# Two pages of values requested together and multiplied back to back in a paged decode

## The chip, the cores and the metric

The kernel runs on one core of a Trainium2 chip. A core has five engines with queues of their own: TensorE (PE, matmuls), VectorE (DVE), ScalarE (ACT), GpSimd (POOL) and SyncE (SP). Each engine takes its instructions in the order of its queue and waits at semaphores for the others. GpSimd and SyncE also issue DMAs here; 16 DMA engines move the data. The metric is the device time of one execution in microseconds.

## The reference

One inference step of a hybrid decoder layer (depth 1, float32), for a prompt of 1024 rows and for 8 samples with one new row each, which share the weights (model width 1024):

```python
q, k, v, logf, u, z = mixer_inputs(rmsnorm(x, g_mix), w_in, b_f, g_sgu_v)
x = x + merge_heads(attention(q, k, v, logf), sgu(u, z, w_s, b_s), g_att_out, g_sgu_out, w_o)
x = x + cross_attend(rmsnorm(x, g_cross), mem_k, mem_v, w_cq, w_co)      # 4 heads, 256 memory rows
x = x + conv_ffn(rmsnorm(x, g_ffn), prev, w_up, conv_w, conv_b, w_down)  # width 2816, gated
y = rmsnorm(x, g_final)
```

The part that matters is the attention of the samples. Each sample has a past of 8192 rows in a paged cache: 64 pages of 128 rows, 8 heads of 64, for keys and for values, 268 MB in all for 8 samples. With the cumulated forget gates as a bias, it is

```python
k_all = concat([k_pool[page_table].reshape(B, past, H, hd), k], axis=1)
v_all = concat([v_pool[page_table].reshape(B, past, H, hd), v], axis=1)
p = softmax(einsum('bqhd,bkhd->bhqk', q, k_all) * hd ** -0.5 + c_q - c_k)
out = einsum('bhqk,bkhd->bqhd', p, v_all)
```

## The kernel before

The prompt's work is the main line. It goes through its stages one after the other (projections, attention, merge and cross-attention "mid", gated MLP "ffn"; the later ones in two halves of 512 rows). Its matmuls are float32 products made from three products of a split (lines 271 to 273), 128 x 512 each.

The samples' work is a second line, `sample()`: first `decode()`, the paged attention, then `sample_rest()`, the samples' own merge, cross-attention and MLP. Both lines are Python generators. The main loop at the end of `build` takes a step of the prompt, adds its weight to a count, and hands out a step of the samples for each `PACE` of that count (`PACE` depends on the stage: 20.0 in the first half's attention, 8.5 in its MLP, 2.5 in the second MLP). So the program order mixes the two. A planner then orders every engine's queue by a simulated time line, with all waits and buffers. `behind(ENG.PE)` adds the edge that the instructions inside may not come ahead of the newest TensorE instruction of the prompt's steps so far (`last`); `tc.issue_after(ins)` is the same for an instruction that is named, and `newest(ENG.PE)` is the TensorE instruction that was written last.

In `decode()` the loop over `g` has 148 steps. A "page" is here one load of 128 partitions x 2048 floats, 1 MB, a sixteenth of a sample's keys or values (4 rows of 512 in each partition). In step `g`, `b, ch = divmod(g, 16)`:

- `kstep(b, ch, ...)` (lines 1338 to 1358): GpSimd requests a page of keys (line 1341, an indirect DMA into a tile of the pool `kv`), VectorE multiplies it by the query (line 1347) and sums within heads into the scores `s` (line 1351).
- At the sample's end come the softmax pieces (`soft_max`, `soft_all`, `soft_exp`, `soft_sum`), spread over the first steps of the next sample.
- `vstep(b, ch, ...)` (lines 1397 to 1415), 18 steps behind the keys (16 and `VLAG` = 2): GpSimd requests a page of values (line 1400, into the same pool `kv`), and a closure `mm` is returned. `mm` multiplies the page (line 1406): four matmuls, one for each of the four rows `j` of a partition, with 32 columns of weights (4 x 8 scores), each in its own group of 32 columns of the array (`tile_position`) and its own 32 partitions of the PSUM tile `dv`, 512 wide. All 16 pages of a sample accumulate into `dv`.
- `vmask` and `vend` take the sum out of `dv`.

The pool `kv` has `NKV` = 4 buffers for keys and values together; whoever asks next gets the buffer that comes free. `dv` has one buffer. The closures wait in the list `pend`. When it holds `VB` = 2, both are called in the step after, the earlier page first, each behind the newest instruction of the prompt; nothing ties the second to the first. In each step one page of values is requested, after the closures that were called in it. So GpSimd's queue alternates: a page of keys, a page of values, a page of keys.

The weights of the prompt come over SyncE's queue into four buffers `wr`; after the decode the samples' weights come over GpSimd's queue into `kv`.

Of the kernel before, what the change touches and what calls it, by code (L numbers as in the profile page):

```python
# [15 lines left out]
ENG = mybir.EngineType  # L16
# [33 lines left out]

NKV = 4
VLAG = 2
VB = 2
MIXR = 1.0
G0R = 0.0
WH = 5
# [23 lines left out]
def build(nc, tc, ctx, a, phases=None):  # L80
# [43 lines left out]
    def KV():  # L124
        return dpool.tile([P, 2048], F32, tag="kv", bufs=NKV, name=nm("kv"))
# [33 lines left out]
    def D2(n=512, dt=F32):  # L159
        return dpool.tile([P, 512], dt, tag="d2", bufs=5, name=nm("d2"))[:, :n]  # L160
# [168 lines left out]
    def newest(e):  # L329

        return next(i for i in reversed(nc.cur_bb.bb.instructions) if i.engine == e)
# [952 lines left out]
    def behind(e):  # L1284

        return tc.issue_after(last[e]) if e in last else nullcontext()


    def decode():
# [77 lines left out]
        def soft_all(b, pm):  # L1367
            ps = MS()
            with behind(ENG.PE):
                nc.tensor.transpose(ps[:8, :P], pm, ident)  # L1370
            with tc.high_priority():
                m1 = sm([8, 1], "m1", 2)
                nc.vector.tensor_reduce(m1, ps[:8, :P], axis=AX.X, op=ALU.max)
                nc.vector.tensor_tensor(mT[:, b : b + 1], m1, snT[:, b : b + 1], op=ALU.max)
                dg = sm([8, 8], "dg", 2)
                nc.vector.tensor_scalar(dg, ident[:8, :8], mT[:, b : b + 1], None, op0=ALU.mult)
            return dg
# [13 lines left out]
        def soft_sum(b, lp):  # L1391
            ps = MS()
            with behind(ENG.PE):
                mmul(ps[:8, :1], lp, ones[:, 0:1], start=True, stop=True)
            nc.vector.tensor_copy(lT[:, b : b + 1], ps[:8, :1])

        def vstep(b, ch, st, dv):
            s = st[1]
            kv = KV()
            nc.gpsimd.indirect_dma_start(kv, None, a["cache_v"], off(kidx[:, b, ch : ch + 1]))  # L1400
            kvv = kv.rearrange("p (k c) -> p k c", c=512)

            def mm():
                with behind(ENG.PE):
                    for j in range(4):
                        mmul(  # L1406
                            dv[32 * j : 32 * j + 32, :],
                            s[:, ch * 4 : ch * 4 + 4, :].rearrange("p k h -> p (k h)"),
                            kvv[:, j, :],
                            start=(ch == 0),  # L1410
                            stop=(ch == 15),
                            tile_position=(0, 32 * j),
                        )

            return mm

        def vmask(b, dv):
            vm = D2()
            with tc.high_priority():
                nc.vector.tensor_tensor(  # L1420
                    vm.rearrange("p (h d) -> p h d", d=64),
                    dv.rearrange("p (h d) -> p h d", d=64),
                    dm8.unsqueeze(2).broadcast_to((P, 8, 64)),
                    op=ALU.mult,
                )
            return vm

        def vend(b, vm):
            ps = MS()
            with behind(ENG.PE):  # L1430
                mmul(ps[:1, :], ones[:, 0:1], vm, start=True, stop=True)
            row = D2()[:1]
            nc.vector.tensor_copy(row, ps[:1, :])
            nc.sync.dma_start(att_d[b : b + 1, :], row)
# [3 lines left out]
        st, A, dt_, pm, dg, lp, dv, vm = ([None] * 8 for _ in range(8))  # L1438
        pend = []
        st[0] = prep(0)  # L1440
        for g in range(8 * 16 + 16 + VLAG + 2):
            b, ch = divmod(g, 16)
            if ch == VLAG + 1 and 2 <= b < 10:
                vend(b - 2, vm[b - 2])
            if ch == 0 and 1 <= b < 9:
                dg[b - 1] = soft_all(b - 1, pm[b - 1])
            if ch == 1 and 1 <= b < 9:
                lp[b - 1] = soft_exp(b - 1, st[b - 1], dg[b - 1])
            if ch == 2 and 1 <= b < 9:
                soft_sum(b - 1, lp[b - 1])  # L1450
            if b < 8:
                kstep(b, ch, st[b])
                if ch == 11:
                    A[b] = gates_scan(b)
                if ch == 13:
                    dt_[b] = gates(b, A[b])
                if ch == 14 and b < 7:
                    st[b + 1] = prep(b + 1)
                if ch == 15:
                    pm[b] = soft_max(b, st[b], dt_[b])  # L1460
            if len(pend) == VB:

                for vb_, vch_, f in pend:
                    f()
                pend.clear()
                if vch_ == 15:
                    vm[vb_] = vmask(vb_, dv[vb_])
            vb, vch = divmod(g - 16 - VLAG, 16)
            if 0 <= vb < 8:
                if vch == 0:  # L1470
                    dv[vb] = DV()
                pend.append((vb, vch, vstep(vb, vch, st[vb], dv[vb])))
            yield 1


# [446 lines left out]
```

## Time and profile before

| | |
|---|---|
| Median of 3 runs | 1874.07 us (1871.21 to 1876.5) |
| The profiled execution | 1881.57 us |
| Its span, first to last instruction | 1879.7 us |
| TensorE busy | 1802.3 us, 96% |
| VectorE, ScalarE, GpSimd busy | 74%, 40%, 26% |
| Granted TensorE clock, mean | 0.982 |
| HBM traffic | 276 GB/s over the span |
| Pages of values multiplied | from 195.8 to 1469.0 us of the span |

How to read the rows: a row of the time line has the start and the length in us, the engine, the line, the operation, the tiles (out<-in), the shapes and the count (neighbours of one kind are merged); in brackets is how long the engine was idle before it and what released it. A row of a stage has its ends, its length, the busy time of each engine (with the count of instructions), the granted clock, the share of time the DMA engines were busy, and GB/s. Groups have, behind the bar, busy time, mean ns of one, and idle time before. A matmul of float32 operands (line 1406) takes two passes and leaves two records. PE is a matmul, PEld the load of its weights, POOLq a queue's own waits.

### The profile page before, as it was taken

What the parts mean: (1) busy time and instruction counts of PE and PEld (TensorE: products, weight loads), DVE (VectorE), ACT (ScalarE), POOL (GpSimd) and SP (SyncE); (2) the same over time, 40 slices, a digit from 0 to 9 for tenths busy, and PEclk for the clock granted to TensorE, in tenths of its full rate; (3) what the DMA queues carried; (4) which work ended last, traced back from release to release, by engine and by line L of the source; (5) the groups of instructions that cost most, each with busy time, mean ns of one, the idle gap of its engine ahead of it and who ended that gap; (6) DMA issues with size and microseconds to landing.
All of it is one profiled execution on the core that took longest, in us unless ns stands there. A gap on an engine that the chain in (4) does not pass through costs nothing.

```text
span 1879.7 us, 24248 instructions
## 1 busy us (share of the span) xinstructions
PE 1802.3 (96%) x9239; PEld 1291.7 (69%) x9239; DVE 1394.2 (74%) x1664; ACT 750.9 (40%) x1363; POOL 480.0 (26%) x437
## 2 busy tenths in 40 slices
PE   8999989878998999999999999999999999999998
PEld 5987666556676667776777776765675668667765
DVE  4788668776687787989989998897965549654344
ACT  6332356565633435333324234235353334232232
POOL 1232333331122332313422323334322111101110
PEclk9999999889998999999999999999999999999999
DMA  8877888784496876759877888889859577667971
GB/s 320 286 261 271 324 324 297 243 263 167 169 376 216 329 268 249 298 197 363 314 274 301 302 316 324 347 325 340 325 220 359 193 282 263 253 219 276 331 246 59
DMA packets 157012, 521.27 MB, mean 277 GB/s; under 512 B 20808, under 2 KB 40520, under 8 KB 124128
## 3 DMA queue, kind: packets, MB, share of 16 engines
q0 software_dynamic: 57168, 341.14, 49.1%
q1 hardware_dynamic: 92816, 165.99, 25.7%
q10 hardware_dynamic: 6912, 12.59, 1.8%
q8 instruction: 73, 1.20, 0.2%
q14 instruction: 43, 0.35, 0.1%
HBM read 495.73 MB, written 23.93 MB: 276 GB/s over the span
## 4 chain that ended last, share of the span: by engine, by line
PE 83%; DVE 5%; DMA 4%; ACT 3%; issue 3%; POOL 1%; SPq 0%; DVEq 0%; POOLq 0%; ACTq 0%
PE ba L271 13%; PE ba L272 12%; PE ba L273 12%; PE bb L271 7%; PE bb L272 7%; PE bb L273 7%; PE dv L1406 6%; DVE kv L1347 1%; PE dv L1656 1%; PE ba L1002 1%; PE ba L1004 1%; DMA kv<-cache_k,kidx 1%; PE bb L788 1%; DVE s L1351 1%; PE ba L1003 1%
## 5 line engine op out<-in xcount | busy, mean ns | idle before, releaser
L234 ACT ACTIVATE wh<-wr 128x1024 fp32r<-128x1024 f32 (+2 forms) x220 | 228.7, 1044 | 518.2 <-PE ba L272 168.5
L235 DVE TENSOR_TENSOR wl<-wr,wh 128x1024 fp32r<-128x1024 f32 (+2 forms) x220 | 262.8, 1200 | 134.0 <-PE ba L273 55.4
L1347 DVE TENSOR_TENSOR kv<-kv,d 128x1024 f32<-128x1024 f32 (+1 forms) x184 | 295.8, 1633 | 24.3 <-DMA kv<-cache_k,kidx 23.6
L1341 POOL DMA_INDIRECT kv<-cache_k,kidx x128 | 177.0, 1383 | 535.0 <-DVE s L1351 262.2
L1351 DVE TENSOR_REDUCE s<-kv 128x16 f32<-128x1024 f32 (+1 forms) x184 | 296.3, 1624 | 0.2
L1400 POOL DMA_INDIRECT kv<-cache_v,kidx x128 | 173.3, 1354 | 404.7 <-DVE s L1351 180.0
L271 PE MATMUL ba<-wh,u 128*128 128x512 f32 (+1 forms) x601 | 229.6, 383 | 4.3 <-DVE u L961 2.5
L272 PE MATMUL ba<-wl,u 128*128 128x512 f32 (+1 forms) x601 | 227.5, 379 | 0.0
L273 PE MATMUL ba<-wh,u 128*128 128x512 f32 (+1 forms) x601 | 224.9, 379 | 0.0
L272 PE MATMUL ba<-u,wh 128*128 128x512 f32 (+2 forms) x520 | 203.1, 391 | 0.0
L271 PE MATMUL ba<-u,wh 128*128 128x512 f32 (+2 forms) x520 | 202.7, 391 | 0.2 <-DVE u L238 0.2
L273 PE MATMUL ba<-u,wl 128*128 128x512 f32 (+2 forms) x520 | 202.1, 389 | 0.0
L271 PE MATMUL bb<-u,wh 128*128 128x512 f32 (+2 forms) x344 | 138.9, 404 | 1.1 <-DVE u L238 1.1
L271 PEld LDWEIGHTS ba<-wh,u 128*128 128x128 f32 x601 | 113.3, 189 | 38.2 <-issue 9.6
L272 PE MATMUL bb<-u,wh 128*128 128x512 f32 (+2 forms) x344 | 137.5, 401 | 1.6 <-DVE u L238 1.6
L1406 PE MATMUL dv<-kv,s 128*32 128x512 f32 x1024 | 135.2, 614 | 3.0 <-DMA kv<-cache_v,kidx 3.0
L273 PE MATMUL bb<-u,wl 128*128 128x512 f32 (+2 forms) x344 | 136.9, 398 | 0.0
L273 PEld LDWEIGHTS ba<-wh,u 128*128 128x128 f32 x601 | 113.0, 188 | 26.7 <-issue 5.0
L272 PEld LDWEIGHTS ba<-wl,u 128*128 128x128 f32 x601 | 113.3, 189 | 22.4 <-issue 1.7
L272 PEld LDWEIGHTS ba<-u,wh 128*128 128x128 f32 x520 | 98.5, 189 | 32.3 <-issue 12.2
L271 PEld LDWEIGHTS ba<-u,wh 128*128 128x128 f32 x520 | 98.3, 190 | 31.5 <-issue 8.4
L273 PEld LDWEIGHTS ba<-u,wl 128*128 128x128 f32 x520 | 98.2, 189 | 27.7 <-issue 8.1
(426 smaller groups left out, 3048.8 us busy)
## 6 DMA issues: line engine op xcount, KB each, us to landing
wr<-w_up SPq DMA_DIRECT2D x88, 512.0 KB
kv<-w_up POOLq DMA_DIRECT2D x22, 1024.0 KB
wr<-w_down SPq DMA_DIRECT2D x40, 512.0 KB
kv<-w_down POOLq DMA_DIRECT2D x11, 1024.0 KB
wr<-w_in SPq DMA_DIRECT2D x16, 512.0 KB
wr<-w_o SPq DMA_DIRECT2D x16, 512.0 KB
wr<-w_cq SPq DMA_DIRECT2D x16, 512.0 KB
wr<-w_co SPq DMA_DIRECT2D x16, 512.0 KB
```

What stands on the lines that cost most here:

```text
L234: nc.scalar.activation(h, src, AF.Copy)
L235: nc.vector.tensor_tensor(l, src, h.bitcast(F32), op=ALU.subtract)
L271: mmul(out, sh, mh, start=(i == 0), stop=False)
L272: mmul(out, sh, ml, start=False, stop=False)
L273: mmul(out, sl, mh, start=False, stop=(i == n - 1))
L788: nc.tensor.transpose(tr[:, c * P : (c + 1) * P], p_[:, kt * P : (kt + 1) * P], ident)
L1002: mmul(pss[i], mh[k][:, tb], wh, start=(k == korder[0]), stop=False)
L1341: nc.gpsimd.indirect_dma_start(kv, None, a["cache_k"], off(kidx[:, b, ch : ch + 1]))
L1347: nc.vector.tensor_tensor(kvv[:, i : i + m, :], kvv[:, i : i + m, :], qb.unsqueeze(1).broadcast_to((P, m, 512)), op=ALU.mult)
L1351: nc.vector.tensor_reduce(s[:, ch * 4 + i : ch * 4 + i + m, :].rearrange("p k h -> p (k h)"), kvv[:, i : i + m, :].rearrange("p k (h d) -> ...
L1400: nc.gpsimd.indirect_dma_start(kv, None, a["cache_v"], off(kidx[:, b, ch : ch + 1]))
L1406: mmul(dv[32 * j : 32 * j + 32, :], s[:, ch * 4 : ch * 4 + 4, :].rearrange("p k h -> p (k h)"), kvv[:, j, :], start=(ch == 0), stop=(ch == ...
```

## The change

`VB` goes. A page pair is now requested in one step: in every second step (`vch` odd) `vstep` is called for pages `vch - 1` and `vch`, one after the other, behind the step's page of keys. In the next step the list is emptied from its end: the later page is multiplied first, behind the newest instruction of the prompt as before, and the earlier page then with an edge to the TensorE instruction just written, the last matmul of the later page. The accumulation in `dv` therefore begins with page 1 and ends with page 14. `dv` is taken in the step in which pages 0 and 1 are requested, and the mask follows pages 15 and 14. The step in which a pair is multiplied is the same as before; page `vch - 1` is requested one step later than before.

```diff
-VB = 2
...
-            def mm():
-                with behind(ENG.PE):
+            def mm(after=None):
+                with tc.issue_after(after) if after else behind(ENG.PE):
                     for j in range(4):
                         mmul(
                             dv[32 * j : 32 * j + 32, :],
                             s[:, ch * 4 : ch * 4 + 4, :].rearrange("p k h -> p (k h)"),
                             kvv[:, j, :],
-                            start=(ch == 0),
-                            stop=(ch == 15),
+                            start=(ch == 1),
+                            stop=(ch == 14),
                             tile_position=(0, 32 * j),
                         )
...
-            if len(pend) == VB:
-
-                for vb_, vch_, f in pend:
-                    f()
-                pend.clear()
-                if vch_ == 15:
-                    vm[vb_] = vmask(vb_, dv[vb_])
+            if pend:
+
+                pend.pop()()
+                pend.pop()(newest(ENG.PE))
+                if vch == 15:
+                    vm[vb] = vmask(vb, dv[vb])
             vb, vch = divmod(g - 16 - VLAG, 16)
-            if 0 <= vb < 8:
-                if vch == 0:
+            if 0 <= vb < 8 and vch % 2:
+                if vch == 1:
                     dv[vb] = DV()
-                pend.append((vb, vch, vstep(vb, vch, st[vb], dv[vb])))
+                pend += [vstep(vb, c, st[vb], dv[vb]) for c in (vch - 1, vch)]
             yield 1
```

## The prediction

> **What bounds the kernel now.** I read the page first (busy time, the chain that ended last, the costliest groups), then busy time by stage, then TensorE's own instructions in order of time around the multiplication of a page of values (line 1406), then GpSimd's requests.
>
> ```profile
> PE 1802.3 (96%) x9239; PEld 1291.7 (69%) x9239; DVE 1394.2 (74%) x1664; ACT 750.9 (40%) x1363; POOL 480.0 (26%) x437
> PE 83%; DVE 5%; DMA 4%; ACT 3%; issue 3%; POOL 1%; SPq 0%; DVEq 0%; POOLq 0%; ACTq 0%
> L1406 PE MATMUL dv<-kv,s 128*32 128x512 f32 x1024 | 135.2, 614 | 3.0 <-DMA kv<-cache_v,kidx 3.0
> ...
> 840.00:960.00 120.00, 120.00 (x550) 85.95 (x550) 108.91 (x97) 37.12 (x56) 40.64 (x27) 1.00 0.85 319
> 960.00:1060.00 100.00, 100.00 (x471) 71.65 (x468) 92.19 (x84) 33.60 (x50) 28.32 (x22) 1.00 0.80 298
> 1160.00:1300.00 140.00, 134.57 (x676) 95.59 (x675) 124.11 (x149) 53.85 (x101) 51.48 (x36) 1.00 0.88 330
> 1380.00:1470.00 90.00, 89.20 (x476) 56.94 (x475) 47.02 (x75) 39.55 (x68) 19.75 (x23) 1.00 0.81 300
> ```
>
> TensorE is busy in 96% of the span and holds 83% of the last chain. In the stage rows the columns after the length are busy PE, PEld, DVE, ACT, POOL, then granted clock, DMA share, GB/s. PE is full from 840 to 1060, nearly full from 1380 to 1470, and lacks 5.4 us from 1160 to 1300. So in most of the time of the decode what TensorE saves comes off the end. The 1024 records of line 1406 are 128 pages of 8 records (four column groups, two passes each), and only 3.0 us of PE idle time stand before them: pages of values practically always arrive in time.
>
> **What the change does on TensorE.** The old code also multiplies two pages in one step, but it does not tie them together. A page that is multiplied alone, and two that stand together:
>
> ```profile
> 847.46 0.40 PE L272 MATMUL ba<-wl,u 128*128 128x512 f32 x1
> 847.78 1.07 PE L1406 MATMUL dv<-kv,s 128*32 128x512 f32 x8
> 848.78 0.50 PE L273 MATMUL ba<-wh,u 128*128 128x512 f32 x1
> 849.12 0.39 PE L271 MATMUL ba<-wh,u 128*128 128x512 f32 x1
> 849.35 0.40 PE L272 MATMUL ba<-wl,u 128*128 128x512 f32 x1
> ...
> 1010.98 0.39 PE L273 MATMUL ba<-u,wl 128*128 128x512 f32 x1
> 1011.30 1.92 PE L1406 MATMUL dv<-kv,s 128*32 128x512 f32 x16
> 1013.15 0.51 PE L271 MATMUL bb<-u,wh 128*128 128x512 f32 x1
> 1013.49 0.40 PE L272 MATMUL bb<-u,wh 128*128 128x512 f32 x1
> ```
>
> Full-array matmuls start 0.23 us apart (849.12 to 849.35). From 847.46 to 849.12 are 1.66 us with one of them and one page between; two ordinary steps would be 0.46, so a page alone costs 1.20. From 1010.98 to 1013.49 are 2.51, so two together cost 2.05. Two alone cost 2.40: each joining saves 0.35 us, the entry into the narrow shape and the way out of it that are gone.
>
> How many pages stand alone shows in the busy time of this line by stage (PE, then PEld):
>
> ```profile
> 1160.00:1300.00 140.00, 17.05 (x128) 2.52 (x128) 1.00 0.88 330
> 1300.00:1400.00 100.00, 11.46 (x80) 1.57 (x80) 0.98 0.82 309
> 1400.00:1470.00 70.00, 18.80 (x144) 3.05 (x144) 1.00 0.84 311
> ...
> 202.52 1.06 PE L1406 MATMUL dv<-kv,s 128*32 128x512 f32 x8
> 1468.52 1.07 PE L1406 MATMUL dv<-kv,s 128*32 128x512 f32 x8
> ```
>
> From 1160 to 1300, 17.05 us for 16 pages is 1.066 each: all alone. From 1400 to 1470, 14 pages alone (14.9 us) and two pairs (3.9 us) make the 18.80. Over all stages the order of time has 73 groups of one page (the first and last are quoted), 24 of two, one of three, and two pairs that a small matmul cuts: 102 groups. After the change the two pages of a step are tied, which leaves 64. So 38 joinings by 0.35 us are **13.3 us of TensorE time**. Of the 73 single groups 35 lie between 760 and 1160 and after 1400, where PE is full or nearly so: 17 joinings, 6 us, that must show. The other 38 lie where PE lacks some per cent (3.9% from 1160 to 1300), and beside small matmuls the switch is a little cheaper. Since even there PE is busy nearly all the time I take **12 us** and keep 6 and 13.3 as bounds.
>
> **The order of the multiplications.** The later page first: PE waits once, for the page that lands last, and the other is there. The flags that open and close the accumulation move with it (pages 1 and 14). No instruction is added or removed, so 0. The masking after page 15 stays behind the same step: 0.
>
> **The requests.** These stand in GpSimd's queue. Now they alternate, keys, values, keys, values; afterwards keys, keys, values, values. 128 requests of each stay, so the issue costs nothing new. What moves is when each is made:
>
> ```profile
> 849.15 0.95 POOL L1400 DMA_INDIRECT kv<-cache_v,kidx  x1 [5.17 <-PE dv L1406]
> 855.21 1.09 POOL L1400 DMA_INDIRECT kv<-cache_v,kidx  x1 [1.93 <-PE dv L1406]
> 863.84 3.12 POOL L1400 DMA_INDIRECT kv<-cache_v,kidx  x1 [0.82 <-PE dv L1406]
> ...
> 871.10 0.94 POOL L1400 DMA_INDIRECT kv<-cache_v,kidx  x1 [0.89 <-PE dv L1406]
> ...
> 1012.66 0.94 POOL L1400 DMA_INDIRECT kv<-cache_v,kidx  x1 [7.63 <-PE dv L1406]
> 1013.91 0.94 POOL L1341 DMA_INDIRECT kv<-cache_k,kidx  x1 [0.30 <-issue]
> 1015.15 0.94 POOL L1400 DMA_INDIRECT kv<-cache_v,kidx  x1 [0.30 <-DVE s L1351]
> 1031.35 0.94 POOL L1400 DMA_INDIRECT kv<-cache_v,kidx  x1 [5.96 <-PE dv L1406]
> ```
>
> A request of values waits for the multiplication that frees a buffer. Where pages are multiplied alone, two requests take 14.7 us (849.15 to 863.84) or 15.9 (855.21 to 871.10); where they already go in pairs, 18.7 us (1012.66 to 1031.35), with the two requests 2.5 us apart. So the old kernel already runs stretches in nearly the new pattern, and PE is as full there. The first page of a pair loses its head start; the price on PE is nothing as long as the planner puts the pair where the later page has landed.
>
> The request of keys that stood behind the first page of values no longer waits for it. All waits of VectorE for keys are 23.6 us; two that stood on the chain that ended last are shown below the total:
>
> ```profile
> L1347 DVE TENSOR_TENSOR kv<-kv,d 128x1024 f32<-128x1024 f32 (+1 forms) x184 | 295.8, 1633 | 24.3 <-DMA kv<-cache_k,kidx 23.6
> ...
> 605.82 2.36 DVE L1347 TENSOR_TENSOR kv<-kv,d 128x1024 f32<-128x1024 f32 x2 [4.00 <-DMA kv<-cache_k,kidx]
> 623.67 1.22 DVE L1347 TENSOR_TENSOR kv<-kv,d 128x1024 f32<-128x1024 f32 x1 [4.33 <-DMA kv<-cache_k,kidx]
> ```
>
> I bound the effect on keys by these two waits, 8.3 us, to either side (they come earlier in GpSimd's queue, but the next two stand behind a pair of values that waits for PE). I take 0, because nothing says which side it falls to. SP's queue (the weights) is not touched; two pages of values in a row, 2 MB, can hold a load of weights back for a moment, which the four raw buffers cover.
>
> **Sum.** The profiled execution took 1881.57 us (span 1879.7), 0.4% above the median of 1874.07. 1881.57 - 12 = 1869.6, a ratio of 0.9936, and by the median 1862 us.
>
> **Rivals.** *Decode falls behind (slower).* With both pages requested together, the loop of a pair is the 13.3 us from request to multiplication (849.15 to its page at 862.47), plus the spacing of requests 1.25 (1012.66 to 1013.91), plus 1.9 for the pair and 1.4 to the next request: 17.8 us, and up to 3.3 more for the second page's transfer (1.05 MB at the 319 GB/s of that stage).
>
> ```profile
> 862.47 1.07 PE L1406 MATMUL dv<-kv,s 128*32 128x512 f32 x8
> ...
> 1848.10 1.02 PE L1709 MATMUL ms<-d,cp 128*8 128x512 f32 x2
> ...
> 1871.66 0.40 PE L273 MATMUL ba<-wh,u 128*128 128x512 f32 x1
> ```
>
> Against 15.9 now, some 30 of the 36 pairs that now run singly lose 2 us or more each, 60 us of delay for the samples. Their last multiplication is at 1848.10 and the prompt's at 1871.66, so 23.6 us are covered; with the 12 gained it decides at 36 us of delay, 1.2 us per pair. If the rest of the samples' path makes up 20 of the 60, then 60 - 20 - 23.6 - 12 is about +4, and if it makes up nothing, +24: I price it at +14, **1888**. For it: the arithmetic above. Against it: the samples' steps are handed out by the prompt's progress, so the loop of 18.7 us from 1012 to 1031 is already fast enough; and from 1470 on the DMA engines have room.
>
> ```profile
> 1470.00:1600.00 130.00, 130.00 (x591) 96.20 (x590) 92.02 (x124) 46.35 (x75) 20.75 (x33) 1.00 0.69 241
> ```
>
> The Trainium skill (Trainium Kernel Development and Optimization, Best Practices) asks for double buffers so that transfers run beside the computing; by it, a pair that holds two of the four buffers until both are multiplied loses that overlap and this rival would come true. The trace does not agree where pairs run now: between 1012.66 and 1031.35 keys are fetched beside the pair. For the second page's transfer the skill (DMA: Bandwidth & Descriptors, Anatomy of one DMA) gives 2.0 us + bytes/436e3, so 2.4 us by that page for one more, which would put the loop at 20.2 us instead of 21.1; no row here times a page's transfer alone.
>
> *TensorE waits for the later page (slower).* TensorE runs in order, so a page that lands after its place in the order stops the prompt's work too.
>
> ```profile
> 1311.44 1.87 PE L1406 MATMUL dv<-kv,s 128*32 128x512 f32 x8 [3.05 <-DMA kv<-cache_v,kidx]
> ```
>
> This is the only such wait now. At 3.05 us each it decides from 4 pairs of 64; with 8 it would be 24 - 12 = +12, **1886**. Against it: one in 128 pages now.
>
> *The gain is covered (same).* Only the joinings in full stages count, 6 us, and a little is lost in other places: -3, **1871**.
>
> **Chances.** The forecast 0.56 (its own range 1855 to 1868, from 6 us to 12 us and half of the 8.3 us on keys more or less); decode behind 0.20; waits of TensorE 0.11; covered 0.13. A measurement of this kernel can tell about 0.3%, 5.6 us, from no change: faster 0.56, same 0.13, slower 0.31. The range for 8 in 10 goes down to 1851 (1874.07 - 13.3 - 8.3 is 1852, and a microsecond for the scatter of the runs) and up to 1887, between the two slower cases, so that about half of their chance is left out.
>
> **What would show it.** In the profile after: 64 groups of 16 records on line 1406, each 1.92 us; its busy time near 64 x 1.92 = 123 us instead of 135.2, PE's total near 1790. Requests of values in twos, 1.25 us apart. Wrong, if PE's idle time grows by more than 12 us: with waits for the values' pages before line 1406 (TensorE waits), or with the samples' last multiplication behind the prompt's (decode behind). If the groups are still 16 records in fewer than 50 places, the tie doesn't hold.

## The result and the profile after

The median of the changed kernel was 1882.55 us against 1874.48 us for the kernel before (seven executions each, side by side): a ratio of **1.0037, 95% interval 1.0022 to 1.0052**. In a second comparison (11 and 23 executions) it was 1883.55 against 1880.34, **1.0023 (1.0011 to 1.0036)**. (The ratios are estimated from all the executions and are not quite the quotients of the two medians.) The change makes the kernel slower by 0.23 to 0.37%. The forecast was 1862 us.

Executions of one kernel scatter by some 0.3% to either side of their median here. The first profiled execution after took 1876.87 us, the quickest of its kernel; the one before took 1881.57 us, longer than any of the seven beside it. These two traces alone would show the wrong sign, so a second trace of the changed kernel (1883.54 us, near its median) stands beside them below.

First, from the page of the profile after, the busy time of the engines, the chain that ended last, and the groups of the keys' and the values' products:

```profile
span 1875.1 us, 24221 instructions
PE 1791.9 (96%) x9239; PEld 1293.9 (69%) x9239; DVE 1391.6 (74%) x1664; ACT 748.7 (40%) x1363; POOL 498.1 (27%) x437
PE 65%; issue 12%; DMA 9%; DVE 7%; POOL 4%; ACT 3%; SPq 0%; POOLq 0%; DVEq 0%; ACTq 0%
L1346 DVE TENSOR_TENSOR kv<-kv,d 128x1024 f32<-128x1024 f32 (+1 forms) x184 | 295.5, 1636 | 37.9 <-DMA kv<-cache_k,kidx 28.9
L1405 PE MATMUL dv<-kv,s 128*32 128x512 f32 x1024 | 131.1, 616 | 5.3 <-DMA kv<-cache_v,kidx 5.3
```

TensorE is busy 10.4 us less than before (1791.9 against 1802.3), yet its share of the last chain fell from 83% to 65%: more of the end is set by issue, DMA and VectorE. (The line numbers are one lower than before. This share alone tells little of the time: below, `tie_only`, as fast as before, has 81%, and `after_ffn`, a faster one, 74%.) The waits for values before the multiplication went from 3.0 to 5.3 us, VectorE's waits for keys from 23.6 to 28.9 us.

The stages shown of before, in the first trace after (busy PE, PEld, DVE, ACT, POOL, then granted clock, DMA share, GB/s):

```profile
840.00:960.00 120.00, 119.64 (x557) 88.16 (x557) 111.90 (x101) 38.08 (x58) 43.98 (x26) 1.00 0.83 305
960.00:1060.00 100.00, 98.44 (x462) 72.25 (x461) 91.01 (x82) 33.07 (x50) 31.91 (x22) 1.00 0.82 302
1160.00:1300.00 140.00, 132.80 (x661) 97.70 (x662) 125.47 (x150) 51.75 (x98) 54.33 (x36) 0.99 0.87 329
1380.00:1470.00 90.00, 89.66 (x487) 61.36 (x484) 48.30 (x79) 37.27 (x66) 18.76 (x21) 1.00 0.81 297
```

TensorE had no idle time at all from 840 to 1060; now it lacks 1.92 us there. From 1160 to 1300 it lacks 7.2 us where it lacked 5.4.

The pair itself, from TensorE's order of time in the first MLP after:

```profile
856.04 0.40 PE L271 MATMUL ba<-u,wh 128*128 128x512 f32 x1
856.37 1.92 PE L1405 MATMUL dv<-kv,s 128*32 128x512 f32 x16
858.23 0.50 PE L272 MATMUL ba<-u,wl 128*128 128x512 f32 x1
858.57 0.39 PE L270 MATMUL ba<-u,wh 128*128 128x512 f32 x1
```

From 856.04 to 858.57 are 2.53 us for one pair and one ordinary matmul, as the 2.51 of the prediction. GpSimd's queue in the same place:

```profile
857.74 0.94 POOL L1340 DMA_INDIRECT kv<-cache_k,kidx  x1 [5.02 <-PE dv L1405]
858.98 1.06 POOL L1399 DMA_INDIRECT kv<-cache_v,kidx  x1 [0.30 <-issue]
860.34 3.63 POOL L1399 DMA_INDIRECT kv<-cache_v,kidx  x1 [0.30 <-issue]
866.28 0.94 POOL L1340 DMA_INDIRECT kv<-cache_k,kidx  x1 [2.31 <-DVE s L1350]
874.66 1.68 POOL L1340 DMA_INDIRECT kv<-cache_k,kidx  x1 [7.43 <-DVE s L1350]
877.12 2.74 POOL L1399 DMA_INDIRECT kv<-cache_v,kidx  x1 [0.78 <-PE dv L1405]
```

Requests of values stand in twos, 1.36 us apart (858.98 to 860.34); the second holds the queue for 3.63 us. The last multiplications of the samples and of the prompt (the same order of time, at the end):

```profile
1843.49 1.02 PE L1707 MATMUL ms<-d,cp 128*8 128x512 f32 x2
...
1867.04 0.40 PE L272 MATMUL ba<-wh,u 128*128 128x512 f32 x1
```

The samples end 23.6 us ahead of the prompt, as before, and the last page of values is multiplied at 1466.4 us (1471.2 in the second trace) against 1469.0: the decode did not fall behind.

To add up where the time lies, I split each span into TensorE's idle time, what it lost to the slower clock (half of its busy time in stretches where half the clock was granted) and the rest, its work at full clock. This is my arithmetic from the records of matmuls and of the clock; the page's busy time sorts a few us otherwise. "Groups" are runs of records of the values' multiplication with nothing between.

| kernel | ratio (95%) | span of the trace | idle | slow clock | work | groups |
|---|---|---|---|---|---|---|
| before | 1 | 1879.7 | 77.4 | 26.7 | 1775.6 | 102 |
| the change, first trace | 1.0037 (1.0022 to 1.0052) | 1875.1 | 83.2 | 22.0 | 1769.9 | 71 |
| the change, second trace | 1.0023 (1.0011 to 1.0036) | 1881.8 | 83.4 | 28.6 | 1769.8 | 71 |
| tie_only | 1.0007 (0.9992 to 1.0023) | 1882.7 | 88.5 | 31.2 | 1762.9 | 70 |
| order_only | 1.0011 (0.9993 to 1.0028) | 1882.3 | 88.5 | 29.9 | 1763.9 | 70 |
| requests_only | 1.0107 (1.0087 to 1.0126) | 1907.6 | 93.2 | 38.6 | 1775.7 | 102 |
| early_pair | 1.0045 (1.0027 to 1.0063) | 1886.5 | 86.8 | 33.4 | 1766.3 | 77 |
| tie_ffn | 0.9994 (0.9983 to 1.0005) | 1880.6 | 75.3 | 32.1 | 1773.1 | 89 |
| after_att | 1.0027 (1.0014 to 1.0041) | 1880.5 | 79.0 | 25.1 | 1776.4 | 98 |
| after_mid | 0.9993 (0.9977 to 1.0009) | 1876.6 | 77.5 | 28.0 | 1771.0 | 91 |
| after_ffn | 0.9978 (0.9965 to 0.9991) | 1870.9 | 78.6 | 21.5 | 1770.8 | 86 |
| after_down | 0.9998 (0.9986 to 1.0009) | 1879.3 | 85.2 | 31.2 | 1762.8 | 71 |
| before_down | 0.9984 (0.9972 to 0.9996) | 1878.8 | 75.2 | 29.8 | 1773.7 | 102 |
| tie_ffn_down | 0.9957 (0.9940 to 0.9974) | 1873.6 | 75.6 | 31.4 | 1766.6 | 89 |
| after_ffn_down | 0.9963 (0.9949 to 0.9978) | 1869.0 | 74.6 | 26.8 | 1767.6 | 86 |
| before_5 | 1.0174 (1.0156 to 1.0192) | 1907.6 | 100.2 | 28.4 | 1779.0 | 88 |
| after_5 | 1.0154 (1.0136 to 1.0173) | 1920.3 | 107.2 | 39.8 | 1773.3 | 66 |

Every ratio is to the kernel before, run on the same chip beside it. A single trace is one execution, so differences of 3 us or less between spans are not read; the columns idle and work are steadier (the two traces of the change agree to 0.2 us in both, and differ by 6.6 us in the slow clock). The trace of `requests_only` took 7 us more than the median of its kernel, that of `after_5` 11 us more.

### The profile page after: what moved, and what is told of

The parts are those of the page before. It is cut to its first block, busy times and chain, and to the rows that moved or that the text cites. A ratio compares the mean times of both kernels' runs of the same rounds, so it can differ in the third digit from the quotient of the medians.

```text
span 1875.1 us, 24221 instructions
## 1 busy us (share of the span) xinstructions
PE 1791.9 (96%) x9239; PEld 1293.9 (69%) x9239; DVE 1391.6 (74%) x1664; ACT 748.7 (40%) x1363; POOL 498.1 (27%) x437
## 4 chain that ended last, share of the span: by engine, by line
PE 65%; issue 12%; DMA 9%; DVE 7%; POOL 4%; ACT 3%; SPq 0%; POOLq 0%; DVEq 0%; ACTq 0%
PE ba L270 10%; PE ba L271 10%; PE ba L272 10%; PE bb L271 5%; PE bb L270 5%; PE bb L272 5%; PE dv L1405 4%; DMA kv<-cache_k,kidx 3%; DMA kv<-cache_v,kidx 3%; DVE s L1350 2%; DVE kv L1346 2%; POOL kv L1399 1%; POOL kv L1340 1%; PE dv L1654 1%; PE bb L803 1%
## 5 line engine op out<-in xcount | busy, mean ns | idle before, releaser
L1340 POOL DMA_INDIRECT kv<-cache_k,kidx x128 | 194.1, 1516 | 621.9 <-DVE s L1350 427.7
L1346 DVE TENSOR_TENSOR kv<-kv,d 128x1024 f32<-128x1024 f32 (+1 forms) x184 | 295.5, 1636 | 37.9 <-DMA kv<-cache_k,kidx 28.9
L1399 POOL DMA_INDIRECT kv<-cache_v,kidx x128 | 178.3, 1393 | 285.5 <-PE dv L1405 208.9
L1405 PE MATMUL dv<-kv,s 128*32 128x512 f32 x1024 | 131.1, 616 | 5.3 <-DMA kv<-cache_v,kidx 5.3
L271 PEld LDWEIGHTS ba<-u,wh 128*128 128x128 f32 x520 | 98.7, 190 | 28.5 <-issue 5.9
L270 PEld LDWEIGHTS ba<-u,wh 128*128 128x128 f32 x520 | 98.6, 190 | 26.7 <-issue 6.3
```

Source lines behind the costliest of these rows:

```text
L270: mmul(out, sh, mh, start=(i == 0), stop=False)
L271: mmul(out, sh, ml, start=False, stop=False)
L1340: nc.gpsimd.indirect_dma_start(kv, None, a["cache_k"], off(kidx[:, b, ch : ch + 1]))
L1346: nc.vector.tensor_tensor(kvv[:, i : i + m, :], kvv[:, i : i + m, :], qb.unsqueeze(1).broadcast_to((P, m, 512)), op=ALU.mult)
L1405: mmul(dv[32 * j : 32 * j + 32, :], s[:, ch * 4 : ch * 4 + 4, :].rearrange("p k h -> p (k h)"), kvv[:, j, :], start=(ch == 1), stop=(ch == ...
```

## The experiments

Three causes stood against each other at the start: the requests in twos (a page, or something behind it, comes late), the tie (TensorE is held to an order that it can't always keep), and the buffers (two of four are taken by a pair). Later ones asked in which stage the loss lies, and what the planner moved elsewhere.

**The two halves, each alone.** `tie_only` keeps the requests as they were and multiplies the later page first with the earlier one tied to it:

```diff
-                for vb_, vch_, f in pend:
-                    f()
-                pend.clear()
+                vb_, vch_, f = pend.pop()
+                f()
+                pend.pop()[2](newest(ENG.PE))
```

The flags move to pages 1 and 14 as in the change. `requests_only` has the change's paired requests, but multiplies the earlier page first and ties nothing (flags at 0 and 15):

```diff
-                pend.pop()()
-                pend.pop()(newest(ENG.PE))
+                pend.pop(0)()
+                pend.pop(0)()
```

`after_again` is the change unaltered, for the second trace. `early_pair` is the change with the pair requested one step earlier, behind the multiplication of the pair before it, so that the pages have a step more to land:

```diff
-            if pend:
+            if pend and vch % 2:
...
-            if 0 <= vb < 8 and vch % 2:
-                if vch == 1:
+            if 0 <= vb < 8 and vch % 2 == 0:
+                if vch == 0:
                     dv[vb] = DV()
-                pend += [vstep(vb, c, st[vb], dv[vb]) for c in (vch - 1, vch)]
+                pend += [vstep(vb, c, st[vb], dv[vb]) for c in (vch, vch + 1)]
```

> The requests as before (one page of values in each step), but the two pages of a step tied, the later one first. Theory A, the later and paired requests cost the time: this one keeps the gain of the joined pages, ratio 0.993 to 0.996, TensorE busy near 1792 us. Theory B, the tie costs the time, because the earlier page's buffer is held until the later one has landed, which delays the requests behind it: 1.000 to 1.005, with more idle time of TensorE and VectorE waiting for pages.

> The requests in pairs as in the changed kernel, but the two multiplications of a step as before: the earlier page first, not tied. Theory A: slower than before by what the requests cost, 1.005 to 1.010 (the loss of the change plus most of the gain that is missing). Theory B: within 0.998 to 1.002, since the buffer of the earlier page comes free as early as before.

> The changed kernel once more, for a second trace beside the first and a narrower interval. If it really is slower, 1.002 to 1.005 of the kernel before; TensorE busy again near 1792 us (the 10 us that the joined pages save are in every run, since the order is fixed), and its idle time between 85 and 95 us instead of 77. If the first comparison was scatter, 0.994 to 0.998.

> The changed kernel, with the pair requested one step earlier: right behind the multiplication of the pair before it, ahead of that step's second page of keys, and multiplied in the same step as before. Theory A, the lost head start costs: 0.993 to 0.998, fewer waits for pages of values. If it is the page of keys that suffers from two pages of values in front of it: 1.003 to 1.008, with VectorE waiting for keys more than the 29 us of the changed kernel. Theory B: as the changed kernel, 1.002 to 1.005.

Measured: the tie alone 1.0007, the requests alone 1.0107, both 1.0023, the pair requested earlier 1.0045. Neither theory holds alone: the tie by itself gains nothing, against theory A, and the requests by themselves cost, against theory B. From the page of `tie_only`, the busy time and the keys' product:

```profile
PE 1794.1 (95%) x9239; PEld 1300.3 (69%) x9239; DVE 1393.0 (74%) x1664; ACT 749.2 (40%) x1363; POOL 482.1 (26%) x437
L1347 DVE TENSOR_TENSOR kv<-kv,d 128x1024 f32<-128x1024 f32 (+1 forms) x184 | 295.6, 1633 | 47.2 <-DMA kv<-cache_k,kidx 40.0
```

The tie does save what the prediction priced: 12.7 us of work (1775.6 to 1762.9) for 32 groups fewer, 0.40 us each. But idle time grows by 11.1 us and the slow clock by 4.5 us, and the time stays. TensorE hardly waits for the values here (0.7 us in all). What grew is found in its waits (engine, line, tile and releaser: total, times, longest). Before:

```profile
PE bb L788 <- ACT t L767: 6.9, 3, 5.7
PE ms L804 <- ACT t L795: 6.2, 4, 2.8
PE ba L1036 <- DVE u L238: 3.7, 4, 1.1
PE dv L1406 <- DMA kv<-cache_v,kidx: 3.0, 1, 3.0
```

and in `tie_only`:

```profile
PE ba L1109 <- ACT t L1097: 5.8, 3, 2.1
PE ba L1036 <- DVE u L238: 5.0, 4, 1.7
PE bb L1036 <- DVE u L961: 4.8, 3, 2.5
PE ba L607 <- DVE u L599: 4.7, 1, 4.7
PE ba L702 <- DMA t<-q_d: 2.8, 1, 2.8
```

These are the prompt's own waits for VectorE, ScalarE and its own loads, each a few us, in other places than before. VectorE meanwhile waits 40.0 us for keys, 16.4 more than before. That a late page of keys holds up the prompt's work behind it in VectorE's queue is an argument; no run isolated it. In the longest of the new waits, 4.7 us until 357.9 us for VectorE's line 599 (the gating unit's input), it is not so: VectorE itself waits there, for a load of the prompt. The request of that load and line 599, before and then in `tie_only`:

```profile
345.75 0.41 SPq L586 DMA_DIRECT2D t<-g_sgu_v  x1
352.91 2.73 DVE L599 SCALAR_TENSOR_TENSOR u<-u,rz,t 128x512 f32<-128x512 f32 x4
```

```profile
345.92 0.35 SPq L586 DMA_DIRECT2D t<-g_sgu_v  x1
356.44 2.74 DVE L599 SCALAR_TENSOR_TENSOR u<-u,rz,t 128x512 f32<-128x512 f32 x4 [4.00 <-DMA t<-g_sgu_v]
```

SyncE makes the request at the same time, but VectorE can begin only 3.5 us later. Between 340 and 352 us the share of the DMA engines is 1.00 to 1.08 in `tie_only` and 0.95 to 1.05 before. The other kernels fall into two groups: TensorE waits at this place for 0.6 to 1.1 us in the seven kernels whose attention goes the old way (before, `before_down`, `after_mid`, `after_ffn`, `after_ffn_down`, `tie_ffn`, `tie_ffn_down`) and for 4.4 to 4.9 us in the change (three traces), `tie_only`, `order_only`, `early_pair` and `requests_only`; in `after_att` it is 1.8 us.

`requests_only` is the slowest of these by far. TensorE's waits in it:

```profile
PE ba L701 <- DMA t<-q_d: 9.4, 1, 9.4
PE dv L1405 <- DMA kv<-cache_v,kidx: 3.2, 1, 3.2
```

The values' pages come in time (3.2 us of waiting, 3.0 before), and VectorE's waits for keys even fall to 13.4 us. But TensorE stands still for 9.4 us until 301.5 us, in the attention, for the prompt's own load of queries. The request of that load, before and in `requests_only`:

```profile
283.36 0.42 SPq L689 DMA_DIRECT2D t<-q_d  x1
```

```profile
281.37 0.42 SPq L688 DMA_DIRECT2D t<-q_d  x1
```

It is made 2 us earlier than before, and yet TensorE can begin with it only at 301.5 us, 20 us later; before, it began at 291.4 without a wait for it. From 280 to 300 us the share of the DMA engines is 1.01 to 1.07 here, and 0.86 to 0.94 from 280 to 290 before. So the load was not requested late: it took longer to land. That the pages on the same DMA engines held it up is my reading. In the second mid stage (1160 to 1400 us of before) the same work takes 11.8 us longer (table by stretches below). Work is unchanged, 102 groups: all of the 28 us by which this trace is longer is idle time and slow clock (15.8 + 11.9). So the requests in twos cost 1.07% by themselves, and with the later page first and tied most of that is not paid.

`early_pair` shows what the keys pay. Its page's row of the keys' product:

```profile
L1346 DVE TENSOR_TENSOR kv<-kv,d 128x1024 f32<-128x1024 f32 (+1 forms) x184 | 295.7, 1634 | 66.4 <-DMA kv<-cache_k,kidx 63.1
```

The values never keep TensorE waiting in it, but the two pages hold two of the four buffers longer, and VectorE waits 63.1 us for keys instead of 28.9. It is slower than the kernel before, and no faster than the change. As I read it, the time given to the values is taken from the keys; whether by the buffers or by the place in GpSimd's queue, where the pair now stands ahead of a page of keys, this run does not tell.

**The order without the tie, the tie in one kind of stage, and a fifth buffer.** `order_only` multiplies the later page first and leaves the earlier one untied; `tie_ffn` does order and tie only while the prompt is in an MLP stage. Requests are as before in both:

```diff
-                for vb_, vch_, f in pend:
-                    f()
+                vb_, vch_, _ = pend[1]
+                turn = phase[0][:3] == "ffn"
+                for n, (_, _, f) in enumerate(pend[::-1] if turn else pend):
+                    f(newest(ENG.PE) if n and turn and True else None, n)
                 pend.clear()
```

(In `order_only` `turn` is always true and `True` is `False`, so the tie is never passed. The flags that open and close the accumulation follow the order.) The fifth buffer for pages needs memory: `before_5` and `after_5` are the two kernels with

```diff
-NKV = 4
+NKV = 5
...
-WH = 5
+WH = 4
 WL = 4
-WR = 4
+WR = 3
```

so with one raw buffer and one high-part buffer of the weights fewer.

> Requests as before, the two pages of a step in the new order (later first) but not tied. It shows what a new order alone does. If a pair falls together almost by itself then, because the earlier page has landed when the later one has: groups and time as with the tie, 1.000 to 1.002, TensorE's work near 1763 us. If any new order of the queues costs some microseconds, whatever it is: 1.001 to 1.004.

> Requests as before, one page of values in each step; the tie (later page first, the other right behind) only in the two MLP stages, where TensorE is full, and not in the attention and mid stages. Theory C, the joined pages are worth their 0.35 us each only where TensorE is full, and in the other stages the new order gives it back as idle time and slow clock: ratio 0.996 to 0.998 (some 16 to 20 joinings, 6 us, and nothing lost before the first MLP stage begins). Theory B, the tie itself costs what it saves because a buffer is held longer: 0.999 to 1.001 here too.

> The kernel before with five page buffers instead of four, paid for with a raw and a high-part weight buffer less (3 and 4 instead of 4 and 5). Only for the comparison with the next one: slower by an unknown amount, 1.00 to 1.03, from the weight buffers.

> The changed kernel with five page buffers and the same weight buffers as the one above; its ratio over that one's is what counts. Theory B, the four buffers are the reason (a pair of values holds two of them until both are multiplied, so that keys come late): the quotient is 0.993 to 0.997, and VectorE waits for keys clearly less than 29 us. If the buffers are not the reason, the quotient stays 1.001 to 1.005.

`order_only` gave 1.0011 and, in TensorE's order of time, this:

```profile
861.35 1.92 PE L1406 MATMUL dv<-kv,s 128*32 128x512 f32 x16
879.57 1.92 PE L1406 MATMUL dv<-kv,s 128*32 128x512 f32 x16
```

It has 70 groups, as many as with the tie, and the same work (1763.9). The order alone joins the pages, and the tie adds nothing to it. As I read it, the earlier page has landed long ago when the planner places the later one, and is placed next.

`tie_ffn` gave 0.9994: idle time 75.3 us, 2.1 less than before, work 2.5 us less, slow clock 5.4 more. No gain that can be told from none, and no loss: by the number that is theory B's range, but its loads at the end stand singly, which takes back a part of what the MLP stages gain (below).

The fifth buffer settled little. With 1.0174 (before) and 1.0154 (the change) the lost weight buffers cost more than the pages' buffer can give; the change beside its own base is 0.998 (the quotient of the two), between the two expected ranges, and the intervals overlap. VectorE's waits for keys rose from 22.0 to 31.1 us in this pair too. Whether the cost of the requests is one of too few buffers was not settled by it.

**The change in one kind of stage at a time.** A flag, set anew at each even page, says whether this pair goes the new way (requested together, later first, tied) or the old one:

```diff
+                if vch % 2 == 0:
+                    two[0] = phase[0][:3] == "ffn"
+                if vch % 2 or not two[0]:
+                    pend += [(vb, c, vstep(vb, c, st[vb], dv[vb])) for c in ((vch - 1, vch) if two[0] else (vch,))]
```

`after_ffn` has the MLP stages, `after_mid` the mid stages, `after_att` the projections and the attention. In all three `dv` is taken with the even page, a step earlier than in the change.

> The whole change, paired requests and tie, but only for pages whose pair falls in the two MLP stages; attention and mid stages as in the kernel before. Theory C, the paired requests cost where the prompt's attention and cross-attention leave TensorE waiting (there the run with the requests alone lost 10 us from 250 to 320 us and 11 us about 1250 us), and nothing in the MLP stages: 0.996 to 1.000. If paired requests cost everywhere alike (20 us over the decode, half of it in the MLP stages, less the joinings): 1.001 to 1.004.

> The whole change only for pairs in the two mid stages (merge, cross-attention). If the second mid stage carries the loss, from 1160 to 1380 us: 1.001 to 1.004 with idle time there above the 9 us of the kernel before. If it gains what its 13 joinings save, 4 us: 0.998.

> The whole change only for pairs that fall into the projections and the attention stages of the prompt; mid and MLP stages as before. If the attention stages carry the loss: 1.002 to 1.005, with more idle time of TensorE between 195 and 560 us than the 32 us of the kernel before (34 from 195 to 550). If they don't, 0.999 to 1.001, since nearly all pairs stand together there already.

Measured 0.9978 (0.9965 to 0.9991), 0.9993 (0.9977 to 1.0009) and 1.0027 (1.0014 to 1.0041). In the MLP stages the change gains: work 4.8 us less, idle time 1.2 more. In the attention stages it loses 5 us by the ratio (4 us between the medians). The stage from 195 to 560, where the attention lies, in the traces of before, `after_att` and `requests_only`, one fence each:

```profile
195.00:560.00 365.00, 331.16 (x1875) 235.23 (x1874) 263.84 (x351) 196.65 (x412) 103.28 (x113) 0.94 0.78 274
```

```profile
195.00:560.00 365.00, 329.60 (x1876) 231.65 (x1875) 261.91 (x351) 195.76 (x411) 107.84 (x114) 0.96 0.78 274
```

```profile
195.00:560.00 365.00, 322.82 (x1812) 226.57 (x1811) 254.48 (x343) 193.98 (x405) 98.35 (x111) 0.93 0.74 259
```

In `requests_only` TensorE leaves 1812 records of matmuls in that time instead of 1875; in `after_att` as many as before.

The prompt's matmuls are the same 7509 in every kernel. To compare like with like I divide each trace at the same ones, those that begin at 195, 400, 560 us and so on in the trace of before; at each of these points the same matmuls of the prompt lie behind in every kernel, and in the kernels of the table each stretch holds the same number of pages of values. Length of each stretch in us, with TensorE's idle time in brackets:

| stretch of before, us | before | tie_only | the change, two traces | requests_only | after_att | after_ffn |
|---|---|---|---|---|---|---|
| 0 to 195 | 195.0 (7.2) | 195.1 (7.2) | 195.4 (7.3), 196.1 (7.2) | 195.8 (7.3) | 195.5 (7.3) | 196.0 (7.4) |
| 195 to 400, attention | 205.0 (20.2) | 209.5 (22.2) | 209.2 (22.9), 210.4 (24.0) | 219.1 (28.5) | 208.4 (21.6) | 202.2 (17.8) |
| 400 to 560, attention | 160.1 (13.6) | 156.7 (14.4) | 155.4 (14.4), 158.0 (14.2) | 158.7 (13.7) | 156.5 (13.8) | 158.0 (14.3) |
| 560 to 760, mid | 199.9 (15.1) | 201.8 (15.8) | 197.0 (13.6), 196.9 (13.7) | 197.2 (13.4) | 200.7 (15.2) | 198.2 (14.6) |
| 760 to 1160, MLP | 400.0 (0.2) | 397.7 (1.6) | 399.4 (2.7), 398.8 (2.0) | 403.2 (2.0) | 400.0 (0.2) | 399.5 (2.8) |
| 1160 to 1400, mid | 239.9 (10.0) | 244.4 (16.0) | 239.9 (12.1), 241.0 (11.7) | 251.7 (16.4) | 240.1 (10.3) | 238.5 (9.6) |
| 1400 to 1600, MLP | 200.2 (0.0) | 197.9 (0.0) | 197.9 (0.0), 197.9 (0.0) | 200.2 (0.0) | 200.1 (0.0) | 197.9 (0.0) |
| 1600 to the end | 279.7 (11.1) | 279.6 (11.2) | 280.8 (10.2), 282.7 (10.6) | 281.8 (12.0) | 279.3 (10.7) | 280.6 (12.0) |

Three readings stand clear of the scatter. From 1400 to 1600, where TensorE never idles, every kernel with the new order there is 2.3 us faster. From 760 to 1160 the order and the tie with the old requests (`tie_only`) gain 2.3 us too, while with paired requests the work falls by 3.0 us and 1.8 to 2.6 us of it come back as idle time. And from 195 to 400 the seven kernels whose attention goes the old way take 201.7 to 205.1 us, but `tie_only`, `order_only`, `after_att` and the three traces with the whole change 208.4 to 210.4: the new order alone, with the requests as before, already costs what the change costs there. From 400 to 560 part comes back (158.0 to 160.3 us the old way, 155.4 to 159.8 the new); over both stretches the loss is 3.6 us by the means of these traces, near the 4 to 5 us measured for `after_att`, though its own trace shows only 1.8 of it.

A part of it is the late load for the gating unit (above). Another candidate is a pair that came late:

```profile
272.18 3.11 PE L1405 MATMUL dv<-kv,s 128*32 128x512 f32 x16 [3.64 <-DMA kv<-cache_v,kidx]
```

This is in the second trace of the change. GpSimd had taken 5.57 us (at 255.17) to issue the first of the two requests, and TensorE waited 3.64 us for the page; `after_att` has the same wait (3.66 us at 271.6). But before has a gap of 5.7 us at nearly the same place (271.2 to 276.95, for ScalarE), so this wait is not simply added. Which waits make up the whole loss of the attention stays open.

**The samples' down projection.** The traces showed one more difference, far from the change. After the decode the samples' weights come through the same pool, one load of 1 MB for two of the four column groups of the array. Before, as a rule two loads are multiplied together:

```profile
1809.61 1.09 PE L1695 MATMUL dv<-kv,d 128*32 128x512 f32 x8
1810.49 1.06 PE L1695 MATMUL ms<-kv,d 128*32 128x512 f32 x8
```

and the busy time of this line alone in that stretch (PE, PEld, clock, DMA share, GB/s):

```profile
1780.00:1850.00 70.00, 13.53 (x88) 3.10 (x88) 1.00 0.58 201
```

After the change most loads (7 of 11, against 3 before) are multiplied singly; its order of time, and the line's busy time:

```profile
1812.49 1.06 PE L1693 MATMUL dv<-kv,d 128*32 128x512 f32 x4
1813.37 1.03 PE L1693 MATMUL ms<-kv,d 128*32 128x512 f32 x4
```

```profile
1780.00:1850.00 70.00, 17.10 (x88) 3.87 (x88) 1.00 0.54 193
```

Two of four column groups cost what four cost: 1.9 us either way (1812.49 to 1814.40, 1809.61 to 1811.55). To see what this is worth, `after_down` and, as a control, `before_down` put that product into closures that run two loads at a time, the later one first:

```diff
...
+            downs.append(down)
+            if len(downs) == 2 or f2 + 2 == NF:
+                while downs:
+                    downs.pop()()
             yield 1
...
```

`tie_ffn_down` has it with `tie_ffn`, and `after_ffn_down` with `after_ffn`, as versions that might beat both kernels.

> The changed kernel, with the samples' down projection at the end taken two loads at a time, the later load first. In the changed kernel most of these loads are multiplied alone, two column groups in use, at 1.9 us each; in the kernel before most stood in twos, four column groups, for the same 1.9 us. If that is where 5 us of TensorE's work came from: 3 to 5 us less than the changed kernel, ratio 0.999 to 1.002, TensorE's work near 1765 us. If not, 1.002 to 1.004 as before.

> The kernel before with the same edit in the samples' down projection, as the control: there only three loads stood alone, so 0 to 2 us: 0.998 to 1.001.

> Requests as before, tie in the MLP stages alone, and the down projection two loads at a time: the version that should beat both if the readings hold. The tie in the MLP stages alone was 0.9994 with the loads standing alone at the end; 3 to 5 us less makes 0.996 to 0.998. If the end does not decide, 0.999 to 1.000.

> The change in the MLP stages alone, and the samples' down projection two loads at a time. If the two add up: 0.9978 less 1 to 3 us, 0.996 to 0.9975. If the shift of the decode splits the loads at the end in another way that the pairing doesn't mend: 0.998 to 1.000.

Measured 0.9998, 0.9984, 0.9957 and 0.9963 (0.9949 to 0.9978). The line's busy time in `after_down`:

```profile
1780.00:1850.00 70.00, 11.43 (x88) 2.92 (x88) 1.00 0.67 238
```

The edit takes 7.0 us of work from the change (1769.8 to 1762.8) and 1.9 from before (1775.6 to 1773.7), a difference of 5.1 us; the busy time of the line alone gives 3.6 (17.10 less 13.53). So 3.6 to 5.1 us of TensorE's work in the change was this tail. Only the change and `tie_ffn` have it: the line is busy 17.09 us in `tie_ffn`, and 13.53, as before, in `tie_only`, `order_only`, `requests_only`, `early_pair` and the three kernels with the change in one kind of stage. In time: the edit gains 0.25% on the second comparison of the change (0.39% on the first) and 0.16% on before, so 0.09 to 0.23% of the loss was the tail. The intervals are about 0.13% to either side each, so the size is rough. The stretch from 1600 us to the end says the like: 1.1 and 3.0 us longer than before in the two traces of the change.

Put together: attention +0.27%, mid -0.07%, MLP -0.22%, which is about nothing, and the split tail, which none of these three kernels has, +0.09 to +0.23%. That makes +0.07 to +0.21% against +0.23 and +0.37% measured. The signs agree; about 0.16% stays unassigned, within what intervals of this size can hide. The two best kernels, `tie_ffn_down` and `after_ffn_down`, use the new order or the whole pairing only in the MLP stages, and beat both kernels: 1871.89 us against 1878.68, and 1872.39 against 1878.57. Of that 0.16% is the edit of the down projection, which the kernel before can have without the pairing; the rest, 0.2 to 0.3%, is the MLP stages.

## Why the prediction was wrong

- **The bound** was right in part. TensorE is busy in 94 to 96% of every span here, but "in most of the time of the decode what TensorE saves comes off the end" was a misreading: of the 77.4 us that TensorE idled before, 58.9 lie in the attention and mid stages (195 to 760 and 1160 to 1400), 805 of the decode's 1273 us. The rows that I had quoted were the fullest ones.
- **A joining saves 0.35 us** was right, even a little low: 12.7 us for 32 groups fewer in `tie_only`. The count was near: 71 groups instead of 64, with 59 of 16 records, because small matmuls still cut some pairs; the line is busy 131.1 us instead of the 123 I expected, 4.4 of it lost to the slower clock, and PE's total is 1791.9 (1790 forecast).
- **"Since even there PE is busy nearly all the time I take 12 us" is the first step that failed.** The work saved came back as idle time and slow clock: work -12.7, idle +11.1, slow clock +4.5 in `tie_only`. By stretches, the two MLP stages became 2.3 us shorter each; in the second mid stage (1160 to 1400) idle time rose by 6.0 us, against 5.0 us of work saved, and the first part of the attention became 4.5 us longer. The bound of 6 us for the full stages alone was near what they gave: 4.6 us in `tie_only`, and a gain of 0.22% (4.4 us) in `after_ffn`.
- **The requests, taken as 0, are the second.** The condition I gave, that the pair stands where the later page has landed, was nearly met (waits for values 3.0 us before, 5.3 and 4.7 in the change), and yet the requests alone cost 1.07%, 20 us by the ratio and outside my 8.3 us. The loss did not come through the values: the longest new wait is for a load of the prompt's own, the queries, requested in time and landed late (9.4 us); which waits make up the rest stays open. I had looked only at keys and at SyncE's weights.
- **The order, taken as 0**, was wrong in kind: it is what joins the pages, not the tie (70 groups in `order_only` and in `tie_only`). And it has a price of its own in the attention, where a load for the gating unit lands late (4.7 us of wait in `tie_only`).
- **What I had no term for:** the tail. A planner orders the whole program, so an edit in the decode split the loads of a product behind the decode: 3.6 to 5.1 us of work.
- **The rivals.** The decode did not fall behind (samples' end 23.6 us ahead of the prompt's, as before), although the time lies near. TensorE's waits for the later page grew by 1.7 to 2.3 us (4.7 and 5.3 against 3.0), not by the 24 priced. "The gain is covered" comes nearest in mechanism, but its 1871 us ends on the wrong side: the covering cost more than the gain. The sign that I had given for being wrong, idle time up by more than 12 us, did not show: it grew by 5.8 and 6.0 us, as much as the work fell (5.7 and 5.8).
- **The forecast's own range**, 1855 to 1868, does not follow from the terms named for it: 12 us and half of 8.3 off 1874 make 1858, 6 off and the half added make 1872. The measured time lies above both.

## What to carry to other kernels

A saving on the busiest engine counts where that engine is full: here 2.3 us of work saved in a full MLP stage were 2.3 us of time. In a stage where it waits at times for others, price the saving at nothing unless the chain of waits says otherwise, and apply the edit in the full stages alone. Add up how much of the span is full before you say "most of it". When two streams share buffers and a queue, do not price a moved request at nothing: ask what the other stream, and the main line's small loads, then wait for. With a planned program, compare places far from the edit too, divide the traces at the same work to do so, and take a second trace before you believe a difference of a few us.

## What the runs showed of the hardware that was not expected

- **The slow clock follows the gaps.** TensorE's granted clock around the wait of 3.64 us, in the second trace of the change (busy PE, PEld, DVE, ACT, POOL, then clock, DMA share, GB/s):

```profile
268.00:272.00 4.00, 0.54 (x3) 0.10 (x1) 2.54 (x5) 3.41 (x6) 1.70 (x1) 1.00 1.02 403
272.00:276.00 4.00, 3.83 (x18) 1.20 (x19) 0.00 (x0) 0.00 (x0) 1.37 (x2) 0.60 1.03 423
276.00:280.00 4.00, 4.00 (x21) 3.25 (x20) 2.49 (x2) 1.19 (x4) 3.97 (x2) 0.98 1.02 414
```

  TensorE is hardly busy from 268 to 272, and for the next 4 us a mean clock of 0.60 is granted: the pair took 3.11 us instead of 1.92. This gap thus cost more than its length. The Trainium skill (TensorE: Matmul & The Clock Gate, HAM oscillation) gives the rule "no PE-idle gaps >~3.4µs"; this gap agrees with it. As a bound it is not sharp here: in the same trace gaps of 1.99 us (until 290.55) and 2.67 us (until 388.2) were followed by a clock of 0.50 and 0.58 in the next 4 us, and one of 2.30 us (until 652.0) by the full clock. Over whole kernels the loss does not simply follow the idle time: 38.6 us with 93.2 us idle in `requests_only`, but 28.4 with 100.2 in `before_5`.
- **Half of the array's columns cost as much as all of them.** Two loads through two column groups each take 1.9 us apiece when multiplied singly, and 1.9 us together.
- **A request can hold GpSimd.** The same indirect request takes 0.94 us in one place and 3.63 (860.34) or 5.57 us (255.17, second trace) in another. A full set of DMA engines alone does not set it: their share was 0.68 from 255 to 261 us, while one of 0.95 us (849.15 of before) stands in a stretch of 0.99. What sets it was not tested.
- **A small load can land late though it is requested in time.** With the DMA engines at a share above 1 a load of queries that was requested at 281.37 us was there for TensorE at 301.5 (`requests_only`); requested at 283.36 in the kernel before, it was in use at 291.4. Which transfers stood in its way was not traced.
